# Norm boundaries of a two-layer hybrid decoder trunk: where the squares of the next norm are added up

## The chip, the cores and the metric

The kernel runs on one core of a Trainium2 chip. The metric is device time in microseconds of one execution. The core has TensorE (matrix products into PSUM), VectorE, ScalarE and GpSimd (elementwise work), and queues that move data between HBM and SBUF. In the rows they are PE, DVE, ACT and POOL; PEld is TensorE's weight load.

## The reference

Two layers over 512 tokens of width 1024, float32. Layer 0 mixes tokens by stick-breaking attention, layer 1 by an indexer-selected sparse attention; each is followed by a gated MLP with a causal depthwise convolution. Every one of the four sub-layers begins with an RMS norm whose scale and shift come from a conditioning vector, and adds its output back through a gate:

```python
def rms_norm(x, g):
    xf = x.astype(jnp.float32)
    y = xf * lax.rsqrt(jnp.mean(xf * xf, axis=-1, keepdims=True) + RMS_EPS)
    return (y * g.astype(jnp.float32)).astype(x.dtype)
...
        h = rms_norm(x, norm_mix[i]) * (1.0 + sc1) + sh1
...
        x = x + g1 * mix
        h = rms_norm(x, norm_ffn[i]) * (1.0 + sc2) + sh2
        x = x + g2 * conv_ffn(h, ffn_w_up[i], ffn_conv_w[i], ffn_conv_b[i], ffn_w_down[i])
```

The case is about the mean of squares between two sub-layers: `x` is complete only when the output projection of the sub-layer before has been added, and the next projection needs the normalised `h`.

## The kernel before

The features lie on the partitions: `x` is eight tiles of 128 features x 512 tokens. A product in near-float32 precision is three matmuls (`mm3`, lines 238 to 241): weights and activations are each split into a rounded high part (ScalarE, line 199 for weights) and a low part (VectorE, line 207 for weights).

A `boundary` joins two sub-layers; there are three (stick-breaking attention to MLP, MLP to sparse attention, sparse attention to MLP). It takes the last quarter of the old output projection and the first projections of the new sub-layer. The tokens are cut in two halves of 256, so that the norm of half 0 is computed by the other engines while TensorE projects half 1.

For each half and each of eight feature tiles m, `out_tile(hf, m)` issues twelve matmuls into a PSUM tile (`pt_l`, two buffers), VectorE adds the result to x (`add_to_x`, line 350: one input from PSUM, one from SBUF), and ScalarE squares the new x into `sqt` (line 276, three buffers). The mean over the features, which lie on partitions, is taken by TensorE: a product with a 128x128 matrix of 1/1024 (`sum_squares`, line 289), which is float32 and shows as two matmul records.

- Half 0: VectorE adds squares 0 to 6 into one tile `sqa` (line 282 a copy, line 284 six adds). Behind tile 0 of half 1 TensorE issues two products, of `sqa` and of square 7.
- Half 1: no adds. TensorE issues one product for each of the eight squares: those of squares 0 to 4 ahead of tiles 3 to 7, those of squares 5 and 6 behind tile 7, that of square 7 in the first new projection behind its k step 1.

The reciprocal root is a ScalarE seed (`norm_seed`, line 306) and a Newton step of three VectorE instructions (lines 312 to 314). Then, for each feature tile, VectorE computes `u` (line 321), ScalarE the high part of h (`norm_hi`), VectorE the low part (line 330). These `norm_ops` of half 0 run inside the loop over half 1, between two weight splits (`split_lo`, line 207); behind the loop two of the four first projections of half 0 (`pt_first`) follow, k step by k step for both, then half 1's norm and the rest.

Within this part the instructions of each engine are issued in the order in which the code is written (the schedule is manual there). An engine takes its own in that order and waits for semaphores of the others. The weights come through one DMA queue well ahead.

Of the kernel before, what the change touches and what calls it, by code (L numbers as in the profile page):

```python
# [21 lines left out]
KT = D // P  # L22
# [93 lines left out]
def kernel_body(ctx, tc, xT, wst, cst, smalls, crow, relb, onehot, outT):  # L116
    nc = tc.nc
    act, dve, pe, pool = nc.scalar, nc.vector, nc.tensor, nc.gpsimd
# [11 lines left out]
    def ptile(shape, name, tag):  # L130
        return banks.tile(shape, F32, name=name, tag=tag, bufs=nbanks[tag])
# [52 lines left out]
    def fetch(i):  # L184
        while pos["f"] <= min(i, len(order) - 1):
            k = order[pos["f"]]
            fetched[k] = chunk_raw(k, width(k))
            pos["f"] += 1

    def split_hi():  # L190
        i = pos["i"]
        if i >= len(order):
            return
        fetch(i + FETCH)
        k = order[i]
        n = width(k)
        raw = fetched.pop(k)
        hi = splits.tile([P, D], F32R, name="whi")
        act.activation(hi[:, :n], raw[:, :n], AF.Copy)  # L199
        pend_lo.append((k, n, raw, hi))  # L200
        pos["i"] += 1

    def split_lo():
        while pend_lo:
            k, n, raw, hi = pend_lo.pop(0)
            lo = splits.tile([P, D], F32R, name="wlo")
            dve.tensor_sub(lo[:, :n], raw[:, :n], hi[:, :n].bitcast(F32))  # L207
            ready[k] = (hi, lo)
# [7 lines left out]
    def chunk(key, ahead=AHEAD):  # L216
        if ahead or key not in ready:
            prefetch(order.index(key) + ahead)
        return ready.pop(key)
# [18 lines left out]
    def mm3(out, whi, wlo, ahi, alo, start, stop):  # L238
        pe.matmul(out, lhsT=whi, rhs=ahi, start=start, stop=False)  # L239
        pe.matmul(out, lhsT=wlo, rhs=ahi, start=False, stop=False)  # L240
        pe.matmul(out, lhsT=whi, rhs=alo, start=False, stop=stop)  # L241
# [30 lines left out]
    sqs = {}  # L272

    def square(f, hf):
        t = npool.tile([P, H2], F32, name="sqt", bufs=3)
        act.activation(t, x[f][:, halves[hf]], AF.Square)
        return t

    def square_add(f, t):
        if f == 0:  # L280
            a = sqs["acc"] = npool.tile([P, H2], F32, name="sqa")
            dve.tensor_copy(a, t)
        else:
            dve.tensor_add(sqs["acc"], sqs["acc"], t)

    def sum_squares(t, start, stop):
        if start:
            sqs["pt"] = ptile([P, H2], "pt_norm", "z")
        pe.matmul(sqs["pt"], lhsT=ones_mean, rhs=t, start=start, stop=stop)
# [3 lines left out]
    def new_h():  # L293
        hcur["h"] = [(hpool.tile([P, S], F32R, name="hhi"), hpool.tile([P, S], F32R, name="hlo"))
                     for _ in range(KT)]

    def norm_scale(l, gcol, sc):
        dve.scalar_tensor_tensor(sfac, mod[l][:, sc * KT:(sc + 1) * KT], 1.0,
                                 sm[:, l * S_L + gcol:l * S_L + gcol + KT], op0=OP.add, op1=OP.mult)
        dve.tensor_scalar(sfac, sfac, -0.5, None, op0=OP.mult)  # L300
# [3 lines left out]
    def norm_seed(hf):  # L304
        ln = rstd[hf] = npool.tile([P, H2], F32, name="ln", bufs=2)
        act.activation(ln, sqs["pt"], AF.Abs_reciprocal_sqrt, bias=eps_c)
        rstd[hf, "ms"] = sqs["pt"]

    def norm_newton(hf):
        ln, ms = rstd[hf], rstd[hf, "ms"]  # L310
        t = npool.tile([P, H2], F32, name="nt")
        dve.tensor_mul(t, ln, ln)
        dve.scalar_tensor_tensor(t, ms, EPS, t, op0=OP.add, op1=OP.mult)
        dve.scalar_tensor_tensor(ln, t, 3.0, ln, op0=OP.subtract, op1=OP.mult)
# [18 lines left out]
    def norm_ops(l, sh, hf):  # L333

        for f in range(KT + 2):
            if f < KT:
                norm_u(hf, f)
                norm_hi(l, sh, hf, f)
            if f >= 2:
                norm_lo(l, sh, hf, f - 2)  # L340
            yield

    def project(out, ck, hs, c=slice(0, S)):
        whi, wlo = ck
        for k in range(KT):
            mm3(out, whi[:, k * P:(k + 1) * P], wlo[:, k * P:(k + 1) * P], hs[k][0][:, c], hs[k][1][:, c],
                k == 0, k == KT - 1)

    def add_to_x(l, g, f, pt, c=slice(0, S)):
        dve.scalar_tensor_tensor(x[f][:, c], pt, mod[l][:, g * KT + f:g * KT + f + 1], x[f][:, c],  # L350
                                 op0=OP.mult, op1=OP.add)
# [11 lines left out]
    def warm(func):  # L363

        act.activation(spare, eps_c, func)

    def boundary(last, O, l, gate, nxt, first):


        cks = [chunk(k, 0) for k in last]  # L370
        nl, gcol, sh, sc = nxt
        new_h()
        norm_scale(nl, gcol, sc)
        fetch(pos["i"] + 1)

        def out_tile(hf, m):
            c = halves[hf]
            whi, wlo = cks[m // 2]
            pt = ptile([P, H2], "pt_l", "tr")
            for k in range(4):  # L380
                w = k * 256 + (m % 2) * P
                mm3(pt, whi[:, w:w + P], wlo[:, w:w + P], O[k][0][:, c], O[k][1][:, c], k == 0, k == 3)
            add_to_x(l, gate, m, pt, c)
            return square(m, hf)

        prev = None
        for m in range(KT):
            t = out_tile(0, m)
            if prev is not None:
                square_add(m - 1, prev)  # L390
            prev = t
            if m == 4:
                warm(AF.Abs_reciprocal_sqrt)
        ops0 = norm_ops(nl, sh, 0)
        pend = []
        for m in range(KT):
            if m == 1:
                sum_squares(sqs["acc"], True, False)
                sum_squares(prev, False, True)
                norm_seed(0)  # L400
            if m >= 3:
                sum_squares(pend[m - 3], m == 3, False)
            pend.append(out_tile(1, m))
            if m == 1:
                norm_newton(0)
            if m in (2, 4):
                split_hi()
            if m in (3, 5):
                split_lo()
            for _ in range((0, 0, 1, 1, 2, 1, 2, 2)[m]):  # L410
                next(ops0, None)
        for m in range(KT - 3, KT - 1):
            sum_squares(pend[m], False, False)
        for _ in ops0:
            pass
        pts = [ptile([P, S], "pt_first", "mm" if i < 3 else "x") for i in range(4)]
        cs = [chunk(k, 0) for k in first[:2]]
        split_hi()
        hs, c = hcur["h"], halves[0]
        for k in range(KT):  # L420
            for i in range(2):
                w = slice(k * P, (k + 1) * P)
                mm3(pts[i][:, c], cs[i][0][:, w], cs[i][1][:, w], hs[k][0][:, c], hs[k][1][:, c], k == 0, k == KT - 1)
            if k == 1:
                sum_squares(pend[KT - 1], False, True)
                norm_seed(1)
                split_lo()
                norm_newton(1)
                split_hi()
        ops1 = norm_ops(nl, sh, 1)  # L430
        for i in range(2, 4):
            for _ in range(2):
                next(ops1, None)
            cs.append(chunk(first[i], 0))
            project(pts[i][:, c], cs[i], hs, c)
        for _ in ops1:
            pass
        return cs, pts
# [24 lines left out]
    def stick_layer(l):  # L463
        with ExitStack() as st:
# [297 lines left out]
            for i in range(HN):  # L762
# [18 lines left out]
                if i == 2:  # L781
# [4 lines left out]
            ada_until(3 * KT)  # L786
            ada_state["cap"] = len(ada_jobs)
            first = boundary([("o", 1, m) for m in range(4)], [O[4 + k] for k in range(4)], l, 2,
                             (l, S_NF, 3, 4), up_first(l))
        return first, man  # L790
# [4 lines left out]
    def ffn_layer(l, first, man):  # L795
        with ExitStack() as st:
# [65 lines left out]
            if l < DEPTH - 1:  # L862
                return boundary(last, O, l, 5, (l + 1, S_NM, 0, 1),
                                [("kw",), ("qi", 0), ("qi", 1), ("qi", 2)]), man
# [3 lines left out]
    def dsa_layer(l, first, man):  # L868
        with ExitStack() as st:
# [203 lines left out]
            with ExitStack() as sa:  # L1073
# [204 lines left out]
                pair_lo()  # L1278
                quarter_proj("do", 0, O[:4], l, 2)
                first = boundary([("do", 1, m) for m in range(4)], O[4:], l, 2, (l, S_NF, 3, 4), up_first(l))  # L1280
        return first, man

# [106 lines left out]
```

## Time and profile before

| | us |
|---|---|
| median of 3 runs (1333.66 to 1335.91) | 1334.76 |
| the profiled execution | 1335.43 |
| its span in the trace | 1333.7 |
| TensorE busy in the span | 1283.2 |
| VectorE busy | 960.9 |
| ScalarE busy | 592.3 |
| GpSimd busy | 22.9 |

The profiled execution is one of those that the chip ran; rows are times from its start. A busy share is an average over the whole span, so a boundary of some 40 us is read from the timelines of that stretch. Matmuls are pipelined: a record lasts longer than the step to the next start, and steps between starts tell what one costs.

### The profile page before, as it was taken

What the parts mean: (1) busy time and instruction counts of PE and PEld (TensorE: products, weight loads), DVE (VectorE), ACT (ScalarE), POOL (GpSimd) and SP (SyncE); (2) the same over time, 40 slices, a digit from 0 to 9 for tenths busy, and PEclk for the clock granted to TensorE, in tenths of its full rate; (3) what the DMA queues carried; (4) which work ended last, traced back from release to release, by engine and by line L of the source; (5) the groups of instructions that cost most, each with busy time, mean ns of one, the idle gap of its engine ahead of it and who ended that gap; (6) DMA issues with size and microseconds to landing.
All of it is one profiled execution on the core that took longest, in us unless ns stands there. A gap on an engine that the chain in (4) does not pass through costs nothing.

```text
span 1333.7 us, 17868 instructions
## 1 busy us (share of the span) xinstructions
PE 1283.2 (96%) x6900; PEld 1069.2 (80%) x6900; DVE 960.9 (72%) x1570; ACT 592.3 (44%) x1051; POOL 22.9 (2%) x22
## 2 busy tenths in 40 slices
PE   2899999999999999999999999989999999999998
PEld 0688878799888888888988877766998888888888
DVE  6987988877877877875778986685676546556653
ACT  4575666454423323443554345573454324324430
POOL 3200000000000000000100000000000000000000
PEclk8999999999999999999999999999999999999999
DMA  7624343423566575554212211112222332333221
GB/s 276 242 82 159 117 146 121 143 75 103 182 227 199 179 244 192 190 180 153 77 51 79 79 48 61 59 41 110 72 87 76 114 105 77 108 106 95 72 87 64
DMA packets 49894, 162.69 MB, mean 122 GB/s; under 512 B 5601, under 2 KB 7905, under 8 KB 49810
## 3 DMA queue, kind: packets, MB, share of 16 engines
q1 hardware_dynamic: 49810, 161.56, 37.5%
q8 instruction: 54, 0.88, 0.3%
q14 instruction: 30, 0.25, 0.1%
HBM read 159.40 MB, written 2.14 MB: 121 GB/s over the span
## 4 chain that ended last, share of the span: by engine, by line
PE 89%; DVE 7%; ACT 2%; issue 1%; DMA 1%; SPq 0%; DVEq 0%; ACTq 0%
PE pt_u L240 11%; PE pt_u L239 11%; PE pt_u L241 11%; PE pt_d L240 5%; PE pt_d L241 5%; PE pt_d L239 5%; PE pt_q L239 2%; PE pt_q L241 2%; PE pt_q L240 2%; PE pt_l L239 2%; PE pt_l L240 2%; PE pt_l L241 2%; PE pt_first L241 2%; PE pt_first L239 2%; PE pt_qk L239 2%; PE pt_first L240 2%
## 5 line engine op out<-in xcount | busy, mean ns | idle before, releaser
L199 ACT ACTIVATE whi<-raw 128x1024 fp32r<-128x1024 f32 (+1 forms) x206 | 205.0, 1002 | 141.2 <-PE pt_d L241 102.6
L207 DVE TENSOR_TENSOR wlo<-raw,whi 128x1024 fp32r<-128x1024 f32 (+1 forms) x206 | 240.1, 1168 | 17.0 <-ACT whi L199 15.9
L240 PE MATMUL pt_u<-hhi,wlo 128*128 128x512 f32 x640 | 249.2, 389 | 0.0
L241 PE MATMUL pt_u<-hlo,whi 128*128 128x512 f32 x640 | 249.2, 389 | 0.0
L239 PE MATMUL pt_u<-hhi,whi 128*128 128x512 f32 x640 | 249.2, 389 | 0.0
L806 ACT ACTIVATE y<-pt_u,sm 128x512 f32<-128x512 f32 x80 | 62.1, 776 | 190.9 <-PE pt_u L241 190.9
L239 PEld LDWEIGHTS pt_u<-hhi,whi 128*128 128x128 f32 x640 | 120.1, 188 | 25.1
L241 PEld LDWEIGHTS pt_u<-hlo,whi 128*128 128x128 f32 x640 | 120.2, 188 | 24.8
L240 PEld LDWEIGHTS pt_u<-hhi,wlo 128*128 128x128 f32 x640 | 120.2, 188 | 24.7
L807 DVE SCALAR_TENSOR_TENSOR y<-pt_u,sm,y 128x511 f32<-128x511 f32 x80 | 59.9, 749 | 98.3 <-ACT y L806 98.3
L248 DVE SCALAR_TENSOR_TENSOR raw<-raw,cond 128x1024 f32<-128x1024 f32 x96 | 120.0, 1261 | 0.0
L241 PE MATMUL pt_d<-actlo,whi 128*128 128x512 f32 x288 | 112.2, 389 | 0.0
L239 PE MATMUL pt_d<-acthi,whi 128*128 128x512 f32 x288 | 112.1, 389 | 0.0
L240 PE MATMUL pt_d<-acthi,wlo 128*128 128x512 f32 x288 | 112.1, 389 | 0.0
L350 DVE SCALAR_TENSOR_TENSOR x<-pt_d,mod,x 128x512 f32<-128x512 f32 x48 | 36.0, 750 | 72.8 <-PE pt_d L241 72.8
L239 PE MATMUL pt_first<-hhi,whi 128*128 128x256 f32 (+1 forms) x224 | 69.4, 310 | 7.6 <-ACT hhi L532 7.6
L241 PE MATMUL pt_first<-hlo,whi 128*128 128x256 f32 (+1 forms) x224 | 68.8, 307 | 8.2 <-DVE hlo L535 7.9
L223 ACT ACTIVATE acthi<-y 128x512 fp32r<-128x512 f32 x44 | 27.8, 632 | 104.3 <-DVE y L825 104.3
L240 PE MATMUL pt_first<-hhi,wlo 128*128 128x256 f32 (+1 forms) x224 | 67.9, 303 | 0.0
L239 PEld LDWEIGHTS pt_d<-acthi,whi 128*128 128x128 f32 x288 | 54.1, 188 | 11.3
L240 PEld LDWEIGHTS pt_d<-acthi,wlo 128*128 128x128 f32 x288 | 54.1, 188 | 11.2
L241 PEld LDWEIGHTS pt_d<-actlo,whi 128*128 128x128 f32 x288 | 54.1, 188 | 11.2
(228 smaller groups left out, 2647.2 us busy)
## 6 DMA issues: line engine op xcount, KB each, us to landing
raw<-wst SPq DMA_DIRECT2D x255, 512.0 KB, 3.7
raw<-wst SPq DMA_DIRECT2D x48, 384.0 KB, 2.9
th<-rb SPq DMA_DIRECT2D x16, 256.0 KB, 3.2
x<-xT SPq DMA_DIRECT2D x8, 256.0 KB, 5.6
outT<-x SPq DMA_DIRECT2D x16, 128.0 KB, 1.7
sm<-smalls SPq DMA_DIRECT2D x1, 248.0 KB, 2.7
cons<-cst SPq DMA_DIRECT2D x1, 192.0 KB, 5.4
oh<-onehot SPq DMA_DIRECT2D x1, 80.0 KB, 1.8
```

Of the source, the lines that this page charges most:

```text
L199: act.activation(hi[:, :n], raw[:, :n], AF.Copy)
L207: dve.tensor_sub(lo[:, :n], raw[:, :n], hi[:, :n].bitcast(F32))
L223: act.activation(hi, src, AF.Copy)
L239: pe.matmul(out, lhsT=whi, rhs=ahi, start=start, stop=False)
L240: pe.matmul(out, lhsT=wlo, rhs=ahi, start=False, stop=False)
L241: pe.matmul(out, lhsT=whi, rhs=alo, start=False, stop=stop)
L248: dve.scalar_tensor_tensor(raw, raw, 1.0, cond, op0=OP.mult, op1=OP.mult, accum_out=dst)
L350: dve.scalar_tensor_tensor(x[f][:, c], pt, mod[l][:, g * KT + f:g * KT + f + 1], x[f][:, c], op0=OP.mult, op1=OP.add)
L806: act.activation(y, pt, AF.Identity, scale=cw[2], bias=sm[:, b + S_CB + c:b + S_CB + c + 1])
L807: dve.scalar_tensor_tensor(y[:, 1:], pt[:, :S - 1], cw[1], y[:, 1:], op0=OP.mult, op1=OP.add)
```

## The change

Both halves now add squares 0 to 6 into `sqa` on GpSimd: the first add takes square 0 (held back) and square 1, so that the copy is gone and six adds are left in each half. Half 1 then has two products with the matrix of ones, as half 0 has; both stand behind k step 1 of the first new projection.

```diff
     def square_add(f, t):
+
         if f == 0:
+            sqs["held"] = t
+        elif f == 1:
             a = sqs["acc"] = npool.tile([P, H2], F32, name="sqa")
-            dve.tensor_copy(a, t)
+            pool.tensor_add(a, sqs.pop("held"), t)
         else:
-            dve.tensor_add(sqs["acc"], sqs["acc"], t)
+            pool.tensor_add(sqs["acc"], sqs["acc"], t)
...
         ops0 = norm_ops(nl, sh, 0)
-        pend = []
+        last0, prev = prev, None
         for m in range(KT):
             if m == 1:
                 sum_squares(sqs["acc"], True, False)
-                sum_squares(prev, False, True)
+                sum_squares(last0, False, True)
                 norm_seed(0)
-            if m >= 3:
-                sum_squares(pend[m - 3], m == 3, False)
-            pend.append(out_tile(1, m))
+            t = out_tile(1, m)
+            if prev is not None:
+                square_add(m - 1, prev)
+            prev = t
...
-        for m in range(KT - 3, KT - 1):
-            sum_squares(pend[m], False, False)
...
             if k == 1:
-                sum_squares(pend[KT - 1], False, True)
+                sum_squares(sqs["acc"], True, False)
+                sum_squares(prev, False, True)
                 norm_seed(1)
```

VectorE in half 0 of the first boundary, before (`x_95` to `x_97` are feature tiles 2 to 4):

```order
L282 COPY sqa<-sqt 128x256
L350 SCALAR_TENSOR_TENSOR x_95<-pt_l,mod_90,x_95 128x256
L284 TENSOR_TENSOR sqa<-sqa,sqt 128x256
L350 SCALAR_TENSOR_TENSOR x_96<-pt_l,mod_90,x_96 128x256
L284 TENSOR_TENSOR sqa<-sqa,sqt 128x256
L350 SCALAR_TENSOR_TENSOR x_97<-pt_l,mod_90,x_97 128x256
```

And now (the line numbers behind the edit are three higher):

```order
L353 SCALAR_TENSOR_TENSOR x_94<-pt_l,mod_90,x_94 128x256
L353 SCALAR_TENSOR_TENSOR x_95<-pt_l,mod_90,x_95 128x256
L353 SCALAR_TENSOR_TENSOR x_96<-pt_l,mod_90,x_96 128x256
L353 SCALAR_TENSOR_TENSOR x_97<-pt_l,mod_90,x_97 128x256
L353 SCALAR_TENSOR_TENSOR x_98<-pt_l,mod_90,x_98 128x256
```

The copy and the adds between the additions to x are gone from VectorE. Its order in half 1 is the same as before.

TensorE behind the last tile of half 1 (`pt_l`) in the first boundary, before, with two products ahead of the new projection:

```order
L240 MATMUL pt_l<-ohi,wlo 128x256
L241 MATMUL pt_l<-olo,whi 128x256
L289 MATMUL pt_norm<-sqt,ones_mean 128x256 x2
L239 MATMUL pt_first<-hhi,whi 128x256
L240 MATMUL pt_first<-hhi,wlo 128x256
```

And now, twelve matmuls further on, behind k step 1 of the two projections:

```order
L240 MATMUL pt_first<-hhi,wlo 128x256
L241 MATMUL pt_first<-hlo,whi 128x256
L292 MATMUL pt_norm<-sqa,ones_mean 128x256
L292 MATMUL pt_norm<-sqt,ones_mean 128x256
L239 MATMUL pt_first<-hhi,whi 128x256
```

The two products ahead of the projection and the five between the tiles are gone; where the product of square 7 stood alone, that of the sum stands ahead of it.

GpSimd from its last work in the first layer to the start of the sparse attention, before:

```order
L568 MEMSET kz_400 64x512
L953 MEMSET work_6110 128x128
L954 COPY work_6110<-cons 128x128
L953 MEMSET work_6113 128x256
L954 COPY work_6113<-cons 128x128
```

And now:

```order
L571 MEMSET kz_400 64x512
L285 TENSOR_TENSOR sqa<-sqt 128x256
L287 TENSOR_TENSOR sqa<-sqa,sqt 128x256 x5
L285 TENSOR_TENSOR sqa<-sqt 128x256
L287 TENSOR_TENSOR sqa<-sqa,sqt 128x256 x5
L285 TENSOR_TENSOR sqa<-sqt 128x256
L287 TENSOR_TENSOR sqa<-sqa,sqt 128x256 x5
L285 TENSOR_TENSOR sqa<-sqt 128x256
L287 TENSOR_TENSOR sqa<-sqa,sqt 128x256 x5
L956 MEMSET work_6110 128x128
```

Four groups of six adds (two boundaries) now stand ahead of the memsets and copies for the indexer; the third boundary's two groups come behind them.

## Rows read from the trace of the kernel before

**Rows 1.** Engine table of the page (busy us, share of the span, instructions).

```profile
PE 1283.2 (96%) x6900; PEld 1069.2 (80%) x6900; DVE 960.9 (72%) x1570; ACT 592.3 (44%) x1051; POOL 22.9 (2%) x22
```

**Rows 2.** Table by stretches: stretch, its length, then busy us (instructions) of each engine.

```profile
core 0: us, PE busy (x) PEld busy (x) DVE busy (x) ACT busy (x) POOL busy (x), PEclk, DMA share, GB/s
269.00:280.00 11.00, 10.78 (x87) 10.73 (x88) 6.16 (x16) 4.69 (x10) 0.00 (x0) 1.00 0.16 48
285.20:295.40 10.20, 10.20 (x77) 9.85 (x76) 10.20 (x22) 7.28 (x16) 0.00 (x0) 1.00 0.36 103
652.30:662.50 10.20, 10.20 (x77) 9.85 (x76) 10.20 (x22) 7.29 (x16) 2.74 (x4) 1.00 0.32 104
959.20:969.40 10.20, 10.20 (x77) 9.85 (x76) 10.20 (x22) 7.28 (x16) 0.00 (x0) 1.00 0.29 104
```

**Rows 3.** Timeline of TensorE, first boundary: start, duration, engine, line, operation.

```profile
283.00 0.28 PE L241 MATMUL pt_l<-olo,whi 128*128 128x256 f32 x1
283.12 0.59 PE L289 MATMUL pt_norm<-sqt,ones_mean 128*128 128x256 f32 x2
283.67 0.28 PE L240 MATMUL pt_l<-ohi,wlo 128*128 128x256 f32 x1
...
294.59 0.28 PE L241 MATMUL pt_first<-hlo,whi 128*128 128x256 f32 x1
294.71 0.59 PE L289 MATMUL pt_norm<-sqt,ones_mean 128*128 128x256 f32 x2
```

**Rows 4.** Timeline of VectorE, half 0 of the first boundary.

```profile
272.40 0.48 DVE L350 SCALAR_TENSOR_TENSOR x<-pt_l,mod,x 128x256 f32<-128x256 f32 x1 [0.62 <-PE pt_l L241]
```

**Rows 5.** Timeline of VectorE, half 1 of the first boundary.

```profile
283.20 0.43 DVE L314 SCALAR_TENSOR_TENSOR ln<-nt,ln 128x256 f32<-128x256 f32 x1
...
285.18 0.48 DVE L350 SCALAR_TENSOR_TENSOR x<-pt_l,mod,x 128x256 f32<-128x256 f32 x1 [0.77 <-PE pt_l L241]
285.59 1.22 DVE L207 TENSOR_TENSOR wlo<-raw,whi 128x1024 fp32r<-128x1024 f32 x1
286.72 0.48 DVE L321 SCALAR_TENSOR_TENSOR u<-ln,sfac,x 128x256 f32<-128x256 f32 x1
...
293.38 0.48 DVE L350 SCALAR_TENSOR_TENSOR x<-pt_l,mod,x 128x256 f32<-128x256 f32 x1
```

**Rows 6.** Timeline of ScalarE, half 1 of the first boundary.

```profile
282.46 0.42 ACT L276 ACTIVATE sqt<-x 128x256 f32<-128x256 f32 x1 [1.51 <-DVE x L350]
...
284.44 1.04 ACT L199 ACTIVATE whi<-raw 128x1024 fp32r<-128x1024 f32 x1
...
293.90 0.42 ACT L276 ACTIVATE sqt<-x 128x256 f32<-128x256 f32 x1 [0.28 <-DVE x L350]
```

**Rows 7.** Timeline of GpSimd, first layer's start.

```profile
30.71 2.24 POOL L525 TENSOR_TENSOR xr<-x,r 128x512 f32<-128x512 f32 x1
32.91 1.26 POOL L525 TENSOR_TENSOR xr<-x,r 128x512 f32<-128x512 f32 x1
```

**Rows 8.** Timeline of VectorE, the same stretch.

```profile
32.96 1.77 DVE L535 TENSOR_TENSOR hlo<-u,hhi 128x512 fp32r<-128x512 f32 x1
...
36.88 2.28 DVE L248 SCALAR_TENSOR_TENSOR raw<-raw,cond 128x1024 f32<-128x1024 f32 x1
...
39.30 0.68 DVE L535 TENSOR_TENSOR hlo<-u,hhi 128x512 fp32r<-128x512 f32 x1
39.90 1.21 DVE L248 SCALAR_TENSOR_TENSOR raw<-raw,cond 128x1024 f32<-128x1024 f32 x1
```

**Rows 9.** Timeline of GpSimd, half 1 of the second boundary.

```profile
659.91 0.77 POOL L954 COPY work<-cons 128x128 f32<-128x128 f32 x1
...
660.88 1.78 POOL L954 COPY work<-cons 128x128 f32<-128x128 f32 x1
```

**Rows 10.** Timeline of VectorE, the same stretch.

```profile
660.45 0.48 DVE L350 SCALAR_TENSOR_TENSOR x<-pt_l,mod,x 128x256 f32<-128x256 f32 x1
...
661.23 1.27 DVE L330 SCALAR_TENSOR_TENSOR hlo<-u,mod,hhi 128x256 fp32r<-128x256 f32 x3
```

## The prediction

> **What bounds the kernel now.** I read the page's engine table first: TensorE is busy 96% of the span, VectorE 72%, GpSimd 2% [rows 1]. So a TensorE instruction taken away pays only where TensorE itself is the last to arrive, and this has to be read at the three boundaries alone. I call the token halves of one boundary half 0 and half 1 and give the times of the first boundary; the other two look the same in the table of rows 2, 367 and 674 us later.
>
> The table by stretches shows two different stages [rows 2]: its first row is half 0, the others are half 1 of the three boundaries. In half 0 TensorE is full and VectorE has 4.8 us of slack in 11. In half 1, from 285.2 to 295.4, both are busy for the whole stretch: VectorE adds to x, computes the new h of half 0 and splits two weight chunks. This second row decides the case.
>
> In the timeline of TensorE the cost of one norm product is visible [rows 3]. Neighbours start 0.12 us apart (283.00, 283.12). From the matmul at 283.00 to the one at 283.67 it would be two such steps, 0.24, without the product at 283.12; it is 0.67. A product costs 0.43 us.
>
> **What is removed.** Half 1 loses eight products of single squares and gets two: six fewer, 6 x 0.43 = 2.58 us of TensorE per boundary, 7.7 us in three. Seven of the eight stood ahead of the first projection (the last of those at m = 7 and behind it), so TensorE arrives there 3.0 us earlier and finds two products at k = 1 instead of one.
>
> Half 0 loses a copy and six adds on VectorE. The addition to x there starts when TensorE ends a tile, after 0.62 us of idle time [rows 4], and a tile has two PSUM buffers. Freeing VectorE there gives nothing. If a GpSimd add were late there, the product at the start of half 1 would wait; the last half-0 square but one has a whole tile (1.44 us) and another one behind it, so I cost this at nothing, and at 0.2 us if I am wrong.
>
> **What gates half 1 once TensorE is fast.** The product at k = 1 needs the square of tile 7, which needs VectorE's addition to x of tile 7, at 293.38 [rows 5]; the square starts 0.04 us after that addition ends and ends at 294.32 [rows 6]. The product starts at 294.71, at once behind the matmul at 294.59: TensorE was last, by 294.71 - 294.36 = 0.35 us. That is all that the square chain leaves to win, unless VectorE's chain gets shorter too.
>
> It hardly does. Ahead of the addition at 285.18 VectorE idled 0.77 us [rows 5]; with one product fewer ahead of that tile 0.43 of it go. But the next instruction, the split at 285.59, needs the high part that ScalarE ends at 284.44 + 1.04 = 285.48 [rows 6], and that depends on nothing that the change hurries. So the chain gains about 0.1 us there, and from there to 293.38 VectorE has no pause. Without any side effect the change would give 0.1 + 0.35 = 0.45 us per boundary, not 2.58.
>
> **What is added.** Six GpSimd adds of 128x256 per half. This trace has GpSimd's multiply of 128x512: 1.26 us where VectorE let it through, 2.24 us where not [rows 7]. VectorE's instructions with two SBUF inputs beside it are stretched: 1.77 instead of 0.68, 2.28 instead of 1.21, by 1.07 to 1.09 us each [rows 8]. So the two exclude each other, and one GpSimd instruction costs VectorE at most 1.07 us at 512 columns; for 256 I take half, an estimate of 0.54. The lower bound is zero: while a GpSimd copy stretched to 1.78 us [rows 9], VectorE's three h instructions beside it took 1.27 us with the starts at their usual steps [rows 10]: GpSimd got in only when they were through. VectorE's addition to x has one SBUF input and one from PSUM; the first GpSimd copy [rows 9], issued at 659.91, ended at 660.68 inside such an addition, which started at 660.45 [rows 10], so I take that as a place where GpSimd may work for free.
>
> In half 0 VectorE has only such additions: no loss. In half 1, add by add:
> - squares 0 and 1: the second ends at 282.88 [rows 6]; GpSimd works to about 283.46, and the Newton step at 283.20 (two SBUF inputs) starts 0.26 late. Through the next addition to x, its square and the high part, the split at 285.59 is late by the same 0.26.
> - square 2: falls beside an idle stretch and an addition: 0.
> - square 3 becomes ready during the split (1.13 us, 285.59 to 286.72 [rows 5]), GpSimd gets in behind it, as in rows 8 behind instructions of that kind: 0.54.
> - square 4 becomes ready among the h instructions and waits, as in rows 9 and 10, for the next addition; that takes 0.40 (the step from 285.18 to 285.59), so 0.14 are left over.
> - square 5: during the second split, 0.54.
> - square 6: gets in at the addition of tile 7 itself, 0 for the gate; the product of the sum is then ready some 0.4 us before that of square 7.
>
> Sum at the addition of tile 7: 0.26 + 0.54 + 0.14 + 0.54 = 1.48 us late, from 293.38 to 294.86. Less TensorE's 0.35 the product at k = 1 comes 1.13 us later than before. Everything behind it (six k steps, the other two projections, the second half) runs on TensorE without a pause as before, and the new h of half 1 shift by the same amount, so the loss stays. Three boundaries: +3.4 us. On the profiled execution's 1335.43 us (span 1333.7) that is 1338.8; it lies 0.67 above the median of the runs, so I forecast 1338.2 us against 1334.76. The six saved products turn into waiting of TensorE ahead of the product of the sum.
>
> The Trainium skill bears on this: "SBUF — State Buffer", section "Who interferes with whom", says that a VectorE instruction with two SBUF inputs and a GpSimd instruction that reads SBUF exclude each other for a whole instruction, and that issue order decides. The stretched multiplies agree; the GpSimd copy passed by three VectorE instructions does not fit it well. By that rule GpSimd would get in behind every instruction, which is the first rival below.
>
> **Rivals.**
> - GpSimd gets in every time (alternation as in rows 7 and 8): four late squares at 0.54 each, 0.26 + 2.16 - 0.35 = 2.07 us per boundary, +6.2, 1341.0 us. Against it: rows 9 and 10.
> - GpSimd gets in only at additions: 0.26 + 3 x 0.14 - 0.35 = 0.33, +1.0, 1335.8 us. For it: rows 10. Against it: the splits, which in the stretch of rows 8 did let it in.
> - GpSimd takes nothing from VectorE at all: 3 x -0.45 = -1.35, 1333.4 us.
> - The change pays in full, because VectorE's chain isn't the gate that I take it for (TensorE stays the last at k = 1): 3 x 2.58 = 7.7 us less, 1327.0 us. It decides from the point where the square of tile 7 is ready 2.2 us earlier than now. For it: TensorE is busy throughout half 1 in rows 2. Against it: VectorE is too, and the addition of tile 7 stands behind all of its work.
>
> **How the numbers follow.** About 0.2%, 2.7 us, is what a measurement of this kernel can tell from no change. Forecast 0.42 (three quarters of it over that bound, the rest under), alternation 0.22, only at additions 0.15, no loss 0.13, full gain 0.08. Slower: 0.32 + 0.22 = 0.54; same: 0.10 + 0.15 + 0.13 = 0.38, of which 0.01 goes to faster, since the no-loss case ends near that bound; faster: 0.08 + 0.01. The range takes in the no-loss case and alternation with some room for a longer GpSimd add, and leaves the full gain out: 1332.8 to 1342.2. The forecast alone would be 1336.5 to 1340.
>
> **What would show it.** Right: in half 1 of each boundary TensorE idle for 1 to 3 us ahead of the product of the sum at k = 1, or of the last square behind it, part of it perhaps already ahead of tiles 5 to 7, whose PSUM buffers VectorE frees; VectorE's splits or the instruction behind them, and the last Newton step, stretched by 0.3 to 0.6 us; GpSimd adds of about 0.7 us in half 0 and of up to 1.8 us in half 1; no product between the tiles of half 1. The place of the k = 1 product after the boundary's first tile says by how much each boundary moved. Wrong: VectorE's durations in half 1 unchanged, or TensorE without idle time there.

## The result and the profile after

The changed kernel took 1342.55 us (median of 6 runs, 1341.77 to 1344.37) against 1335.34 for the kernel before on the same chip (1333.66 to 1336.63): ratio 1.0057, 95% interval 1.0046 to 1.0069. It is slower, as forecast, but by 7.2 us where 3.4 were forecast, and 0.35 us beyond the end of the range. The rival "GpSimd gets in every time" (1341.0) was the better forecast.

The engine table of the page, to set against [rows 1]:

```profile
PE 1280.9 (95%) x6864; PEld 1064.9 (79%) x6864; DVE 961.1 (72%) x1549; ACT 592.4 (44%) x1051; POOL 48.2 (4%) x58
```

TensorE and VectorE have fewer instructions. Yet VectorE is as busy as before: what it lost in copies and adds came back in longer instructions. The timeline of VectorE in half 1 of the first boundary (start, duration in us) shows which; everything up to here starts 1.02 us later than in the trace of before:

```profile
284.22 0.78 DVE L317 SCALAR_TENSOR_TENSOR ln<-nt,ln 128x256 f32<-128x256 f32 x1
...
286.89 1.23 DVE L207 TENSOR_TENSOR wlo<-raw,whi 128x1024 fp32r<-128x1024 f32 x1 [0.61 <-ACT whi L199]
288.03 0.96 DVE L324 SCALAR_TENSOR_TENSOR u<-ln,sfac,x 128x256 f32<-128x256 f32 x1
288.92 0.47 DVE L353 SCALAR_TENSOR_TENSOR x<-pt_l,mod,x 128x256 f32<-128x256 f32 x1
289.31 0.47 DVE L324 SCALAR_TENSOR_TENSOR u<-ln,sfac,x 128x256 f32<-128x256 f32 x1
289.70 0.47 DVE L333 SCALAR_TENSOR_TENSOR hlo<-u,mod,hhi 128x256 fp32r<-128x256 f32 x1
290.10 0.96 DVE L324 SCALAR_TENSOR_TENSOR u<-ln,sfac,x 128x256 f32<-128x256 f32 x1
...
292.91 0.96 DVE L324 SCALAR_TENSOR_TENSOR u<-ln,sfac,x 128x256 f32<-128x256 f32 x1
...
295.37 0.95 DVE L324 SCALAR_TENSOR_TENSOR u<-ln,sfac,x 128x256 f32<-128x256 f32 x1
...
296.63 0.47 DVE L353 SCALAR_TENSOR_TENSOR x<-pt_l,mod,x 128x256 f32<-128x256 f32 x1
```

Five instructions are stretched: the Newton step from 0.43 to 0.78, and four `u` from 0.48 to 0.95 or 0.96, each by one GpSimd add that became ready during the instruction in front of it. Two of the four come behind a weight split (288.03, 292.91), two in the middle of the h instructions (290.10, 295.37). The timeline of GpSimd for the last two:

```profile
289.99 0.79 POOL L287 TENSOR_TENSOR sqa<-sqa,sqt 128x256 f32<-128x256 f32 x1 [1.27 <-ACT sqt L276]
...
295.31 0.72 POOL L287 TENSOR_TENSOR sqa<-sqa,sqt 128x256 f32<-128x256 f32 x1 [1.73 <-ACT sqt L276]
```

The addition of tile 7 starts at 296.63. In [rows 5] it stood at 293.38, with the 1.02 us at 294.40: it is 2.23 us late. By the steps between starts, 0.28 of this is the split at 286.89 (285.59 before, with the 1.02 us 286.61) and 1.95 the four `u`. The table of what TensorE waited for in this boundary (engine, line, waited for: us in total, times, longest):

```profile
PE pt_l L239 <- DVE x L353: 2.2, 3, 0.8
PE pt_norm L292 <- POOL sqa L287: 1.0, 1, 1.0
PE pt_norm L292 <- ACT sqt L276: 0.9, 1, 0.9
```

Before, the same table has one line, 0.7 us for the addition to x. So TensorE now waits 4.1 us in all: the 2.58 us of the saved products turned into waiting, and more came on top. Of the two waits at k = 1 the one that ends last is that for the square of tile 7 (timeline of TensorE, with the idle time ahead of each product):

```profile
296.09 0.70 PE L292 MATMUL pt_norm<-sqa,ones_mean 128*128 128x256 f32 x2 [1.04 <-POOL sqa L287]
297.67 0.70 PE L292 MATMUL pt_norm<-sqt,ones_mean 128*128 128x256 f32 x2 [0.88 <-ACT sqt L276]
```

The sum from GpSimd is there 1.6 us before that square, which hangs on VectorE's addition at 296.63.

How much longer a boundary became is read between two ScalarE instructions that every kernel here has: its first square, and the first instruction that reads a finished first projection. Before, the first boundary runs from 269.20 to 309.25, 40.06 us unrounded. After:

```profile
270.23 0.81 ACT L276 ACTIVATE sqt<-x 128x256 f32<-128x256 f32 x2 [2.27 <-DVE x L353]
...
312.31 0.76 ACT L809 ACTIVATE y<-pt_first,sm 128x512 f32<-128x512 f32 x1
```

| length of the three boundaries | first | second | third |
|---|---|---|---|
| before | 40.06 | 40.12 | 40.12 |
| after | 42.09 | 42.12 | 42.16 |

That is 2.03 + 2.00 + 2.04 = 6.07 us. Outside the boundaries the two profiled executions (spans 1333.7 and 1342.4) differ by another 2.6 us, in three places: 0.46 us in favour of the changed kernel at the start, and 1.5 us against it at each of two stretches in which the granted clock of TensorE stood at half (1.2 of 2.4 GHz), far from any boundary. The table by stretches shows one, first before, then after (the last three figures are PEclk, DMA share and GB/s):

```profile
64.00:68.00 4.00, 3.75 (x32) 3.74 (x33) 3.79 (x6) 3.93 (x8) 0.00 (x0) 1.00 0.53 162
```

```profile
64.00:68.00 4.00, 4.00 (x23) 4.00 (x23) 3.37 (x6) 3.82 (x7) 0.00 (x0) 0.57 0.53 172
```

The profiled execution of the changed kernel took 1344.3 us, 1.75 above its median, so the medians hold less of this. Of their 7.2 us, 6.1 are the boundaries; the other 1.1 us I do not settle.

### The profile page after: what moved, and what is told of

It reads as the page before. It is cut to its first block, busy times and chain, and to the rows that moved or that the text cites. A ratio compares the mean times of both kernels' runs of the same rounds, so it can differ in the third digit from the quotient of the medians.

```text
span 1342.4 us, 17845 instructions
## 1 busy us (share of the span) xinstructions
PE 1280.9 (95%) x6864; PEld 1064.9 (79%) x6864; DVE 961.1 (72%) x1549; ACT 592.4 (44%) x1051; POOL 48.2 (4%) x58
## 4 chain that ended last, share of the span: by engine, by line
PE 87%; DVE 9%; ACT 2%; issue 1%; DMA 1%; SPq 0%; DVEq 0%; ACTq 0%
PE pt_u L241 11%; PE pt_u L240 11%; PE pt_u L239 11%; PE pt_d L241 5%; PE pt_d L240 5%; PE pt_d L239 5%; PE pt_q L239 2%; PE pt_q L241 2%; PE pt_q L240 2%; PE pt_qk L239 2%; PE pt_qk L241 2%; PE pt_qk L240 2%; PE pt_first L241 2%; PE pt_first L239 2%; PE pt_l L239 2%; PE pt_first L240 2%
```

## The experiments

Theories: **A**, GpSimd's adds and VectorE's instructions with two SBUF inputs exclude each other, and VectorE's chain gates half 1. **B**, a sum from GpSimd reaches TensorE late. **C**, TensorE gates. **D**, GpSimd's slow hand-over (0.74 us for an add, and a wait at each end), not the exclusion, is what costs. Boundaries are measured as above; ratios are against the kernel before on the same chip.

| kernel | boundaries, us longer than before | median, us | before, us | ratio (95%) |
|---|---|---|---|---|
| half0_gpsimd | -0.01, -0.01, -0.01 | 1335.43 | 1335.59 | 0.9999 (0.9990 to 1.0008) |
| half1_gpsimd | 2.07, 2.05, 2.08 | 1343.96 | 1335.59 | 1.0064 (1.0051 to 1.0077) |
| memsets | -0.20, -0.27, -0.20 | 1335.68 | 1335.59 | 1.0000 (0.9992 to 1.0009) |
| onepass_products | -1.08, -1.08, -1.09 | 1332.42 | 1335.59 | 0.9971 (0.9960 to 0.9981) |
| half1_vectore | 2.77, 1.27, 2.79 | 1341.90 | 1336.35 | 1.0044 (1.0029 to 1.0058) |
| copies | 0.31, 0.28, 0.30 | 1337.28 | 1336.35 | 1.0010 (1.0001 to 1.0018) |
| half_width | 0.65, 0.64, 0.64 | 1338.18 | 1336.35 | 1.0017 (1.0008 to 1.0026) |
| onepass_reordered | -1.52, -1.40, -1.53 | 1331.57 | 1336.35 | 0.9969 (0.9957 to 0.9980) |
| triple_adds | 8.37, 8.33, 7.79 | 1361.51 (one run) | 1335.44 | |

**One half at a time.** `half0_gpsimd` is the kernel before with this edit:

```diff
         if f == 0:
-            a = sqs["acc"] = npool.tile([P, H2], F32, name="sqa")
-            dve.tensor_copy(a, t)
-        else:
-            dve.tensor_add(sqs["acc"], sqs["acc"], t)
+            sqs["held"] = t
+        elif f == 1:
+            a = sqs["acc"] = npool.tile([P, H2], F32, name="sqa")
+            pool.tensor_add(a, sqs.pop("held"), t)
+        else:
+            pool.tensor_add(sqs["acc"], sqs["acc"], t)
```

> Half 0 adds its squares on GpSimd, half 1 has the eight single products as before. Theory A (GpSimd's adds exclude VectorE's instructions with two SBUF inputs, and only half 1 has those): no change against before, 1335.3 us, additions to x in half 0 at their usual 0.48 us. Rival B (any sum that comes from GpSimd reaches TensorE late): TensorE waits ahead of the product of the sum behind tile 0 of half 1, up to 1 us per boundary, 1338.

`half1_gpsimd` is the changed kernel with half 0's copy and adds on VectorE again.

> Half 0 as before on VectorE, half 1 as in the changed kernel. Theory A: the whole loss is here, each boundary 2.0 us longer, 1341.4 us in a run without extra clock stretches. Rival B: about half of the loss, 1338.

The whole loss is in half 1. In half 0 the adds run beside nothing but additions to x, which keep their 0.48 us; the timeline of VectorE in `half0_gpsimd`, at a time when GpSimd adds at 276.28 and 277.40 for 0.73 us each:

```profile
276.26 0.48 DVE L352 SCALAR_TENSOR_TENSOR x<-pt_l,mod,x 128x256 f32<-128x256 f32 x1 [0.96 <-PE pt_l L241]
277.70 0.48 DVE L352 SCALAR_TENSOR_TENSOR x<-pt_l,mod,x 128x256 f32<-128x256 f32 x1 [0.95 <-PE pt_l L241]
```

Freed of its own adds there (idle 0.95 instead of 0.62 [rows 4]), VectorE gives nothing back either, as forecast. B is out for half 0: TensorE's one wait in that boundary is the old one, 0.6 us for an addition to x.

**The same places without a read.** `memsets` puts GpSimd memsets where the changed kernel has half 1's adds:

```diff
-                square_add(m - 1, prev)
+                square_add1(m - 1, prev)
...
+        if f == 1:
+            pool.memset(sqs.pop("held"), 1.0)
+        pool.memset(t, 1.0)
+        sqs["acc"] = t
```

> The adds of half 1 are replaced by GpSimd memsets of the square tiles, at the same places and behind the same squares; the sum of half 1 is left out. They read no SBUF. Theory A: no instruction of VectorE is stretched, the chain is as before, and only what TensorE was late is won, 0.45 us per boundary, 1334.0 us. Rival B (the loss is the wait of TensorE for GpSimd's last result): a memset is shorter than an add by some 0.4 us, so the boundary stays about 1.6 us longer than before, 1340.

The timeline of VectorE, across a memset at 287.47:

```profile
287.21 0.48 DVE L342 SCALAR_TENSOR_TENSOR hlo<-u,mod,hhi 128x256 fp32r<-128x256 f32 x1
287.61 0.48 DVE L333 SCALAR_TENSOR_TENSOR u<-ln,sfac,x 128x256 f32<-128x256 f32 x1
```

No instruction is stretched, and the loss is gone; B had 1340. But six products fewer and no exclusion give only 0.20 to 0.27 us per boundary, so VectorE's chain is the gate. About half of the 0.45 that I had expected is missing. TensorE waits 0.91 us for the last square, and the product behind this wait takes 0.35 us to the next start (293.74, then 294.09) where the one at 294.71 in [rows 3] took 0.24 (next start 294.95): 0.11 lost. Another 0.06 goes at the square of tile 7, which starts 0.10 us behind the end of the addition where it was 0.04 before.

```profile
293.74 0.70 PE L301 MATMUL pt_norm<-sqt,ones_mean 128*128 128x256 f32 x2 [0.91 <-ACT sqt L276]
294.09 0.47 PE L239 MATMUL pt_first<-hhi,whi 128*128 128x256 f32 x1
```

**TensorE relieved without GpSimd.** `onepass_products` is the kernel before with squares and ones in the format of the other matmuls (the squares are rounded to it):

```diff
+    ones_r = cpool.tile([P, P], F32R, name="ones_mean")
+    ones_mean = ones_r.bitcast(F32)
...
-        t = npool.tile([P, H2], F32, name="sqt", bufs=3)
+        t = npool.tile([P, H2], F32R, name="sqt", bufs=3)
...
-        pe.matmul(sqs["pt"], lhsT=ones_mean, rhs=t, start=start, stop=stop)
+        pe.matmul(sqs["pt"], lhsT=ones_r, rhs=t, start=start, stop=stop)
```

> The kernel before, with squares and the matrix of ones in the one-pass format of the other matmuls, so that a norm product costs about 0.12 us of TensorE instead of 0.43; GpSimd has no part in it. Theory A (VectorE's chain gates half 1): only 0.62 us ahead of half 0's norm and the 0.35 to 0.45 us by which TensorE was last, about 1.0 us per boundary, 1332.2 us, with TensorE waiting in half 1. Rival C (TensorE gates): ten products at 0.31 us per boundary, 9.3 us in all, 1326.

A product now takes one step of 0.12 us on TensorE (timeline):

```profile
283.59 0.28 PE L290 MATMUL pt_norm<-sqt,ones_mean 128*128 128x256 f32 x1
283.71 0.28 PE L240 MATMUL pt_l<-ohi,whi 128*128 128x256 f32 x1
```

Ten of them save 3.1 us per boundary; the boundary is 1.08 us shorter, close to the 1.0 that A gave, and TensorE waits 1.1 us for squares. C is out.

**Can the chain be shortened?** `onepass_reordered` adds to it:

```diff
-            if m in (3, 5):
+            if m == 3:
                 split_lo()
...
-        for k in range(KT):
-            for i in range(2):
+        for i in range(2):
+            for k in range(KT):
                 ...
-            if k == 1:
+            if i == 0:
```

> One-pass products, and VectorE's second weight split of half 1 moved behind the new h, with the first two projections one after the other and the product of square 7 between them. If VectorE's chain is what gates half 1 (theory A), the addition of tile 7 comes 1.13 us earlier and the boundary is about 2 us shorter than before, 1329.5 us. If TensorE gates (rival C), nothing beyond the one-pass products, 1332.4 us.

The addition of tile 7 does come 1.14 us earlier than in `onepass_products`, but the boundary is only 0.3 to 0.4 us shorter in the trace, not 1. TensorE had 1.1 us of waiting for squares left there; this is gone, and 0.5 us of waiting for the split that was moved has come in its place (table of waits; the first line is the old wait for an addition to x):

```profile
PE pt_l L240 <- DVE x L351: 0.6, 1, 0.6
PE pt_first L241 <- DVE wlo L208: 0.5, 1, 0.5
```

Both one-pass kernels are faster than before and after, by 0.3% against before. Whether the reordering adds to that, the two intervals, from different jobs, don't tell.

**What an add costs on VectorE itself.** `half1_vectore` gives half 1's copy and adds to VectorE (half 0 on GpSimd):

```diff
+        if f == 0:
+            a = sqs["acc"] = npool.tile([P, H2], F32, name="sqa")
+            dve.tensor_copy(a, t)
+        else:
+            dve.tensor_add(sqs["acc"], sqs["acc"], t)
```

> Half 1 adds its squares on VectorE itself (a copy and six adds of 0.42 us), GpSimd adds only in half 0. Theory A (an add on GpSimd takes 0.48 us of VectorE wherever VectorE needs two SBUF inputs, so it is no cheaper than an add on VectorE): a copy and five adds stand ahead of the addition of tile 7, about 2.3 us less the 0.2 to 0.35 that TensorE was late: 2.0 us per boundary, 1341.5 us, as the changed kernel. Rival D (what costs in the changed kernel is GpSimd's slower hand-over, 0.74 us and a wait at each end): VectorE's own adds should lose less than half of it, 1338.

The second boundary, in which the granted clock stayed at 1.00, is 1.27 us longer than before, less than GpSimd's 2.00: neither A's 2.0 nor D's less than half of it. A was wrong in the price of an add on VectorE. The copy and the first two adds fell into VectorE's idle time at the start of half 1, and behind that an add costs 0.33 us from start to start, not the 0.42 of its record (timeline of VectorE):

```profile
287.43 0.41 DVE L294 TENSOR_TENSOR sqa<-sqa,sqt 128x256 f32<-128x256 f32 x1
287.76 0.48 DVE L331 SCALAR_TENSOR_TENSOR u<-ln,sfac,x 128x256 f32<-128x256 f32 x1
```

Three such adds make the addition of tile 7 1.1 to 1.2 us late, against 2.23 in the changed kernel. So the difference between the two kernels stands in VectorE's chain, where an add on GpSimd takes 0.48 us and an add on VectorE itself 0.33, and D, by which it would lie in the hand-over, is not needed for it. Handing the adds over does not relieve VectorE in half 1.

The other two boundaries are 1.5 us longer still. In them the granted clock of TensorE stood at half (1.2 of 2.4 GHz) for a while from the end of the wait for the sum on, in the second it did not (tables by stretches, first and second boundary; at a clock of 0.63 in 4 us TensorE loses 4 x 0.37 = 1.5 us):

```profile
296.00:300.00 4.00, 4.00 (x23) 3.82 (x22) 3.56 (x8) 2.36 (x4) 0.00 (x0) 0.63 0.22 37
```

```profile
664.00:668.00 4.00, 2.93 (x21) 2.83 (x22) 3.66 (x8) 3.40 (x6) 0.00 (x0) 1.00 0.04 15
```

That wait is 2.2 us in one piece in all three boundaries, so it alone does not explain the fall of the clock, and I leave its cause open:

```profile
PE pt_norm L299 <- DVE sqa L294: 2.2, 1, 2.2
```

**One input, and half the columns.** `copies` has `pool.tensor_copy(a, t)` and `pool.tensor_copy(sqs["acc"], t)` for the adds; `half_width` adds only the first 128 columns:

```diff
+        c = slice(0, H2 // 2)
...
+            pool.tensor_add(sqs["acc"][:, c], sqs["acc"][:, c], t[:, c])
```

> The adds of half 1 are GpSimd copies of the square tiles, same places, same waits; the sum of half 1 is left out. One SBUF input instead of two. A1 (any GpSimd read of SBUF gets in ahead of the next VectorE instruction and holds it for its length): the five VectorE instructions are stretched by about 0.2 us each, boundary 0.8 us longer than before, 1337.8 us. A2 (a copy passes beside VectorE, as the three h instructions of rows 10 suggested): no stretch, boundary 0.2 us shorter, 1335.

> The adds of half 1 take 128 of the 256 columns, the rest is a memset once; the sum of the other 128 tokens of half 1 is left out. Theory A with a hold that goes with the columns: stretches of about 0.25 us instead of 0.48, boundary about 0.9 us longer than before, 1338.2 us. A hold of fixed length: as the changed kernel, 2.0 us per boundary, 1341.5.

The timelines of GpSimd and VectorE where they meet among the h instructions, in `copies`, then in `half_width`:

```profile
289.34 0.41 POOL L297 COPY sqa<-sqt 128x256 f32<-128x256 f32 x1 [1.31 <-ACT sqt L276]
289.41 0.61 DVE L334 SCALAR_TENSOR_TENSOR u<-ln,sfac,x 128x256 f32<-128x256 f32 x1
```

```profile
287.90 0.51 POOL L298 TENSOR_TENSOR sqa<-sqa,sqt 128x128 f32<-128x128 f32 x1 [1.28 <-ACT sqt L276]
288.01 0.68 DVE L335 SCALAR_TENSOR_TENSOR u<-ln,sfac,x 128x256 f32<-128x256 f32 x1
```

From 0.47: 0.14 for a copy of 256 columns, 0.21 for an add of 128, 0.48 for an add of 256. The hold goes with the columns and with what GpSimd reads. A2 is out. A1 is right in kind, with 0.14 for its 0.2 on the four `u`; the Newton step keeps its 0.43, and the boundary is 0.3 us longer for its 0.8. In `half_width` it is 0.64 longer, where a hold of fixed length had 2.0.

The hold is shorter than GpSimd's record. From the start of the held instruction the record has 0.34 us left in `copies` (0.14 held), 0.40 in `half_width` (0.21 held) and 0.68 at the add of 289.99 in the changed kernel (0.49 held by the steps): VectorE is let through some 0.2 us before the record ends in all three. Why is not shown.

**Which instructions let GpSimd in?** `triple_adds` is the changed kernel with each add of half 1 issued three times:

```diff
                 square_add(m - 1, prev)
+                if m > 1:
+                    for _ in range(2):
+                        pool.tensor_add(sqs["acc"], sqs["acc"], prev)
```

> Each of the six adds of half 1 is issued three times (the sum of half 1 is then too large), so that GpSimd has an add waiting nearly all through half 1 and meets every kind of VectorE instruction. If GpSimd gets in ahead of any instruction with two SBUF inputs, the low-part instructions (hlo) are stretched by 0.48 us as the u instructions are, some 16 stretches per boundary, and the boundary is some 7 us longer than before. If it never gets in ahead of a low-part instruction, as rows 9 and 10 would have it, only u, the splits and the Newton steps are stretched, by 0.48 us each, at most 10 per boundary, about 4 us longer; the additions to x keep 0.48 us in both cases.

The timeline of VectorE with GpSimd always waiting:

```profile
289.35 0.47 DVE L353 SCALAR_TENSOR_TENSOR x<-pt_l,mod,x 128x256 f32<-128x256 f32 x1
289.75 0.55 DVE L324 SCALAR_TENSOR_TENSOR u<-ln,sfac,x 128x256 f32<-128x256 f32 x1
290.22 0.96 DVE L333 SCALAR_TENSOR_TENSOR hlo<-u,mod,hhi 128x256 fp32r<-128x256 f32 x1
291.10 0.95 DVE L324 SCALAR_TENSOR_TENSOR u<-ln,sfac,x 128x256 f32<-128x256 f32 x1
291.98 0.94 DVE L333 SCALAR_TENSOR_TENSOR hlo<-u,mod,hhi 128x256 fp32r<-128x256 f32 x1
292.84 0.47 DVE L353 SCALAR_TENSOR_TENSOR x<-pt_l,mod,x 128x256 f32<-128x256 f32 x1
```

GpSimd gets in ahead of every instruction with two SBUF inputs, the low parts included (0.94 to 0.96). The addition to x is never longer. The instruction behind it loses only 0.08 us: GpSimd's add runs through the addition. Of the boundary's 8 us a part is the product of the sum, which waits for GpSimd's last add (4.8 us here), so only the stretches are read from this run.

## Why the prediction was right in sign and wrong in size

- **The saved products**: right. 0.43 us each left TensorE, and none reached the end: TensorE waits instead.
- **VectorE's chain as the gate**: right, shown by `memsets` (it gains no more than 0.27 us per boundary, with nothing held) and by `onepass_products` (3.1 us less of TensorE, 1.08 gained).
- **Half 0 at nothing**: right (`half0_gpsimd`).
- **The hold**: right in size. 0.54 was estimated from half of a 512-column multiply (by the prediction's own rows that is 1.09, not "at most 1.07"); it measured 0.48. GpSimd's adds took up to 1.08 us in half 1, where up to 1.8 was expected.
- **The Newton step, "late by the same 0.26" at the split**: the step was held 0.35 for 0.26, and the split is 0.28 late. The prediction had itself found 0.1 of slack ahead of this split and did not take it off here; the two errors nearly cancel.
- **"Square 4 ... waits, as in rows 9 and 10, for the next addition", 0.14**: this step failed. The add got in at the very next instruction, for 0.48. I had generalised from one copy that was passed by three low-part instructions, against 8 stretches in the first layer. `triple_adds` shows that low parts let GpSimd's adds in like all others, and `copies` that a copy of 256 columns holds VectorE for only 0.14. For the 128 columns of rows 9 half of that would be 0.07, an estimate. Rows 10 show not even that, and why is open.
- **"Square 6: gets in at the addition of tile 7 itself", 0**: failed by the same reading. The add started at 295.31, with a `u` and a low part still ahead of that addition, got in at the `u` and cost 0.48.
- **TensorE's 0.35**: too large. Between the 2.23 us by which tile 7's addition is late and the 2.03 of the boundary lie 0.20. As in `memsets`, the product behind a wait takes 0.11 longer (297.67, next start 298.02), and the square starts 0.10 behind the addition instead of 0.04.

With every add at the measured hold the sum is 0.28 + 4 x 0.48 - 0.20 = 2.00 us per boundary, against 2.00 to 2.04 measured. The two failed terms are 0.34 + 0.48 = 0.82 of the missing 0.9 (1.13 forecast, 2.03 measured). The first rival's 2.07 has the right mechanism, but that it lies so near is in part luck: its holds are 0.24 too long in sum, its 0.35 for TensorE is 0.15 too large.

The rule of the Trainium skill ("SBUF — State Buffer", "Who interferes with whom") gave that rival. The traces agree with it for adds (0.48 held), for memsets (nothing held) and for additions to x, which it lets pass (0.48 us as ever); "for a whole instruction" is not what they show, since VectorE is let through some 0.2 us before GpSimd's record ends.

Still open: why the copies in [rows 9] took up to 1.78 us (in the changed kernel the same three stand behind the adds and take 0.29 to 0.43), and the 1.1 us of the medians outside the boundaries.

## What to carry to other kernels

Before work goes from VectorE to GpSimd, look at what VectorE does at that time: beside instructions that read two SBUF operands an add on GpSimd took more of VectorE (0.48 us) than an add there (0.33); beside instructions that read PSUM and one SBUF operand it cost VectorE nothing. A saved matmul counts only if TensorE is the last to arrive; where two engines are both full in a stretch, follow the dependence at its end (here the last square) back to the engine on which it queues. When one row seems to show an exception to an exclusion that many others show, price the forecast with the many.

## What was not expected of the hardware

A GpSimd add of 128x256 that is ready gets in ahead of the very next two-input VectorE instruction, even when these stand back to back at steps of 0.39 us, and holds it for 0.48 us; a copy of the same size holds it 0.14, an add of half the width 0.21, a memset not at all. VectorE goes on some 0.2 us before GpSimd's record of the add or copy ends. A float32 product that TensorE starts behind a wait takes 0.11 us longer to the next start than one in a full stream (0.35 and 0.24).
